# Input projection of a hybrid decoder layer: x stored by quarters, its loads and combinations in the order of the products, four sums on GpSimd

## The chip, the cores and the metric

One core of one Trainium2 chip runs the whole kernel as one program. The metric is device time in microseconds of that core. Its engines are called as the profile calls them: PE is TensorE (PEld its weight loads), DVE is VectorE, ACT is ScalarE, POOL is GpSimd, SP is SyncE, which here issues every DMA.

## The reference

The reference is one decoder layer for 1024 prompt tokens and 8 sample tokens that share the weights. All of it is float32. The change touches the first product, the projection of x into all branches, and two cache copies at the end of the decode branch:

```
z = x @ w_in                       # (1032 tokens, 1024) x (1024, 7680)
xr, yr, q, k, v, xq, g = split(z)  # conv + RG-LRU, window attention, memory attention, gates
...
s_win_k = concat(win_k, k)[:, -128:]   # 8 samples: the cached rows moved up by one, the new row last
s_win_v = concat(win_v, v)[:, -128:]
```

After z come the three branches, a gated merge, an output projection with LayerNorm, and a SwiGLU block with LayerNorm.

## The kernel before, in words

**Projection.** z is made transposed, 60 tiles of 128 columns, taken in 30 units of two tiles (the list UNITS, numbered from 0: unit 0 is "xq 0", unit 1 "lru 0", unit 2 "gate 0", unit 3 "xq 1"; the queue of side work runs beside them). A unit multiplies a weight matrix of 2 x 2 blocks (two tiles, each cut in two along the contraction) with x cut in 2 x 2 blocks (halves kh of the contraction, halves th of the tokens). It uses a seven-product scheme in place of eight products: seven sums of weight blocks (`fast_quarter`, lines 190 to 201; tiles us, u) times seven sums of x blocks (`combos`, lines 157 to 183; tiles t, th, tl). The tokens of a half are done in two parts p = 0 and 1 of 258, so a "quarter" of x is 4 x 258 numbers in each of 128 partitions, 516 KB. Each operand is held as two float32r numbers, high and low: ACT casts the high part (line 71), DVE subtracts for the low part (line 72). A product is then three matmuls for each of four contraction steps (lines 212 to 214), 12 matmuls of 128 x 258, and a unit has 7 x 2 x 12 = 168.

**Start of the projection.** `project` loads the four weight blocks of unit 0 (line 82, tiles ur), then calls `combos` for p = 0 and for p = 1. Each call loads its four quarters of x (line 153) from the tensor xT, whose rows are laid out by 128-row tiles, so a quarter comes in runs of 258 numbers (1032 bytes). It then makes t1 = b11 - b12, t2 = -t1 - b22, t3 = b22 - b12, t4 = -t2 - b21 on DVE (lines 170, 173, 177, 181), and splits b11, t1, t2, b21, t3, b22, t4 into high and low, the operands of products 0 to 6. The order of calls is the order in which a scheduler at build time weighs them; it decides each engine's fixed order of instructions by its own estimate of times and by the free buffers of the pools (9 buffers for tiles of the size of a quarter, 6 for raw weight blocks). On the chip each engine then runs its list strictly in that order and waits on semaphores. At most eight of SP's DMAs are under way: a ninth waits for the one eight places before it.

**Side work.** When a unit is finished, its results go on: an xq unit is split and stored (lines 298 to 306) and starts a generator for the sample tokens' memory attention (`dec_mem`, lines 709 to 748: products of cached keys on DVE, line 724); an lru unit starts the conv and recurrence (`lru`, lines 633 to 697: convolution on DVE, lines 646 and 647; casts and gate matmuls by thirds of the tokens, tiles xch, xcl, g; activations, line 662). `pump` lets one step of each run beside each product of the later units.

**Cache copies.** `dec_win_scores` (line 768), traced long after the projection, issues two copies within DRAM of 1016 KB each (line 777: o_swk from cwk, o_swv from cwv). They depend on nothing, so the scheduler puts them early in SP's list. `tc.issue_after(i)` is a block that queues what is traced in it on the engine of instruction i behind i; `self.last_mm` is the last matmul traced.

Of the kernel before, what the change touches and what calls it, by code (L numbers as in the profile page):

```python
# [11 lines left out]
F32R = mybir.dt.float32r  # L12
AF = mybir.ActivationFunctionType
ALU = mybir.AluOpType
# [4 lines left out]
P = 128  # L19
D = 1024  # L20
KT = D // P
TP = 1024
NB = 8
T = TP + NB
CH = ((0, 384), (384, 384), (768, 264))
NM = 256
# [7 lines left out]
HT = T // 2  # L34
QN = T // 4
QS = 272
# [17 lines left out]
class Builder:  # L54
# [94 lines left out]
    def x_quarter(self, kh, th, p):  # L149

        t = self.zt(f"x{kh}{th}{p}")
        t0 = HT * th + QN * p
        self.x_loaded = self.nc.sync.dma_start(t.rearrange("p (k n) -> p k n", k=4),
                                               self.io["xT"][:, 4 * kh:4 * kh + 4, t0:t0 + QN]).ins
        return t

    def combos(self, p, quarter):

        nc = self.nc
        b11, b21, b12, b22 = quarter(0, 0, p), quarter(1, 0, p), quarter(0, 1, p), quarter(1, 1, p)  # L160
        out = []

        def keep(src, i):
            hi, lo = (self.tp.tile([P, 4, QS], F32R, tag="t", name=f"t{e}{i}_{p}", bufs=28) for e in "hl")
            self.split(hi[:, :, :QN], lo[:, :, :QN], src.rearrange("p (k n) -> p k n", k=4))
            out.append((hi, lo))

        keep(b11, 0)
        t1 = self.zt(f"t1_{p}")
        nc.vector.tensor_sub(t1, b11, b12)  # L170
        keep(t1, 1)
        t2 = self.zt(f"t2_{p}")
        nc.vector.scalar_tensor_tensor(t2, t1, -1.0, b22, op0=ALU.mult, op1=ALU.subtract)
        keep(t2, 2)
        keep(b21, 3)
        t3 = self.zt(f"t3_{p}")
        nc.vector.tensor_sub(t3, b22, b12)
        keep(t3, 4)
        keep(b22, 5)
        t4 = self.zt(f"t4_{p}")  # L180
        nc.vector.scalar_tensor_tensor(t4, t2, -1.0, b21, op0=ALU.mult, op1=ALU.subtract)
        keep(t4, 6)
        return out

    def fast_load(self, u, src0, src1):
        h = D // 2
        return {"raw": [[self.half_raw(src[:, e * h:(e + 1) * h], h, f"ur{u}_{j}{e}") for e in range(2)]
                        for j, src in enumerate((src0, src1))], "u": u}

    def fast_quarter(self, st, i):  # L190

# [64 lines left out]
    def project(self):  # L256

        nc, io, tc = self.nc, self.io, self.tc
        self.qdc = self.cst.tile([P, KT * NB], F32, name="qdc")
        self.qds = self.cst.tile([P, KT * NB], F32, name="qds")  # L260
        self.kd = self.cst.tile([P, 2 * NB], F32, name="kd")
        self.vd = self.cst.tile([NB, 256], F32, name="vd")
        self.lru_setup()
        self.side, self.pumped = (deque(), deque()), 0
        n = len(UNITS)
        finish = [Finish(self, kind, j) for kind, j in UNITS]
        st = {}

        def load(u):
            a, b = finish[u].rows  # L270
            st[u] = self.fast_load(u, io["win"][a], io["win"][b])

        load(0)
        ts = [self.combos(p, self.x_quarter) for p in range(2)]
        with tc.issue_after(self.x_loaded):
            self.load_consts()
            self.load_lru()
        self.lru_consts()
        todo = [(u, i) for u in range(n) for i in range(7)]
        ahead = 3  # L280
        for u, i in todo[:ahead]:
            self.fast_quarter(st[u], i)
        for k, (u, i) in enumerate(todo):
            if i == 1 and u + 1 < n:
                load(u + 1)
            if k + ahead < len(todo):
                v, j = todo[k + ahead]
                self.fast_quarter(st[v], j)
            self.fast_step(st[u], i, ts, finish[u])
            self.pump()  # L290
            if i == 6:
                del st[u]
        while any(self.side):
            self.pump()
        nc.sync.dma_start(self.scr["c"][:, :, TP:T], self.cdec)
        self.store_lru()
# [471 lines left out]
    def dec_win_scores(self):  # L768

        nc, io, dp = self.nc, self.io, self.dp  # L770
        krow = dp.tile([NB, 256], F32, tag="krow", name="krow", bufs=1)
        ps = self.bank("mm", "dkt")
        for m in range(2):
            nc.tensor.transpose(ps[:NB, m * P:(m + 1) * P], self.kd[:, m * NB:(m + 1) * NB], self.ident)
        nc.scalar.copy(krow, ps[:NB, :256])
        for name, cache, row in (("o_swk", "cwk", krow), ("o_swv", "cwv", self.vd)):
            nc.sync.dma_start(io[name][:, 0:P - 1, :], io[cache][:, 1:P, :])
            nc.sync.dma_start(io[name][:, P - 1, :], row)
        qb = dp.tile([P, P], F32, tag="dqb", name="dqb", bufs=1)
        nc.gpsimd.memset(qb, 0.0)  # L780
        q5 = qb.rearrange("p (b j e g) -> p b j e g", b=NB, j=2, e=2)
        self.dec_heads(q5, self.qds.rearrange("p (m b) -> p m b", b=NB), True)
        sc = self.bank("mm", "dss")[:, :P]
        for b in range(NB):
            kk = dp.tile([P, 2, P], F32, tag="dk", name=f"dsk{b}", bufs=2)
            nc.sync.dma_start(kk, io["cwkT"][b])
            nc.gpsimd.tensor_copy(kk[:, :, 0], self.kd.rearrange("p (m b) -> p m b", b=NB)[:, :, b])
            for j in range(2):
                o = slice(b * 16 + 8 * j, b * 16 + 8 * j + 8)
                nc.tensor.matmul(sc[:, o], kk[:, j, :], qb[:, o], start=True, stop=True)  # L790
        self.dec_sc = dp.tile([P, P], F32, tag="dss", name="dss", bufs=1)
        nc.scalar.copy(self.dec_sc, sc)
# [307 lines left out]
class Finish:  # L1100
# [40 lines left out]


_INS = {
    "xT": (P, KT, T), "memT": (P, KT * NM), "wmk": (KT, P, D), "wmv": (8, P, D), "win": (60, P, D),
    "wbr": (24, P, D), "wout": (KT, P, D), "wgu": (2 * NF, P, D), "wdn": (KT, P, NF * P), "wlru": (KT, P, 256),
    "vec": (P, V_N), "cst": (P, P + 256), "scv": (P, KT, 3, NB), "sh": (P, KT, NB), "cwk": (NB, P, 256),
    "cwv": (NB, P, 256), "cwkT": (NB, P, 2, P), "cmk": (NB, NM, D), "cmvT": (NB, D, NM),
# [8 lines left out]
def _pack(i):  # L1156
    import numpy as np

    f = {k: np.asarray(v) for k, v in i.items()}
# [11 lines left out]
    o = {}  # L1171
    x = np.concatenate([f["x_prompt"].reshape(TP, D), f["x_sample"].reshape(NB, D)], axis=0)
    o["xT"] = x.T.reshape(KT, P, T).transpose(1, 0, 2)
    o["memT"] = f["mem_prompt"].reshape(NM, D).T.reshape(KT, P, NM).transpose(1, 0, 2).reshape(P, KT * NM)
    wkv = f["w_mem_kv"][0]
    o["wmk"] = mtiles(wkv[:, :D])
    o["wmv"] = np.concatenate([halves(wkv[:, D + 256 * n:D + 256 * (n + 1)]) for n in range(4)], axis=0)
    win = f["w_in"][0]
# [64 lines left out]
```

## Time and profile before

| | |
|---|---|
| median of 3 runs | 2022.97 us (2019.1 to 2027.29) |
| the profiled execution's own time | 2021.07 us |
| its span in the trace | 2018.5 us |
| unit 0's first matmul starts at | 10.00 us |
| unit 2's first matmul starts at | 68.79 us |
| granted TensorE clock, mean over the span | 0.993 |

A row of a timeline gives start, duration, engine, line, operation, output and inputs, shape, count, and in brackets how long the engine was idle before it and what ended that idle time. A row of the groups gives busy time and mean duration of one. A row of the windows gives, for a stretch of time, the busy time and number of operations of each engine, then the granted clock of TensorE, the share of time in which the DMA engines moved data, and GB/s. Matmul durations in the rows overlap; start to start is what counts.

### The profile page before, as it was taken

What the parts mean: (1) busy time and instruction counts of PE and PEld (TensorE: products, weight loads), DVE (VectorE), ACT (ScalarE), POOL (GpSimd) and SP (SyncE); (2) the same over time, 40 slices, a digit from 0 to 9 for tenths busy, and PEclk for the clock granted to TensorE, in tenths of its full rate; (3) what the DMA queues carried; (4) which work ended last, traced back from release to release, by engine and by line L of the source; (5) the groups of instructions that cost most, each with busy time, mean ns of one, the idle gap of its engine ahead of it and who ended that gap; (6) DMA issues with size and microseconds to landing.
All of it is one profiled execution on the core that took longest, in us unless ns stands there. A gap on an engine that the chain in (4) does not pass through costs nothing.

```text
span 2018.5 us, 35388 instructions
## 1 busy us (share of the span) xinstructions
PE 1960.8 (97%) x13732; PEld 1928.1 (96%) x13732; DVE 1198.8 (59%) x2569; ACT 878.8 (44%) x1922; POOL 112.7 (6%) x160
## 2 busy tenths in 40 slices
PE   6999999999999899999999999999999999999997
PEld 5999999999999898988999999999999999999996
DVE  8797789777766555399776559523222332233457
ACT  5456555646655455298673344322111221122324
POOL 1000010100000000022110003100000000000001
PEclk9999999999999999999999999999999999999998
DMA  5555544462233777567425241111211111111102
GB/s 196 186 170 176 184 155 163 150 225 103 95 132 122 248 226 225 158 168 208 136 85 171 88 136 29 42 42 49 57 42 43 48 54 45 55 42 43 57 29 84
DMA packets 143513, 235.42 MB, mean 117 GB/s; under 512 B 17281, under 2 KB 73681, under 8 KB 143313
## 3 DMA queue, kind: packets, MB, share of 16 engines
q1 hardware_dynamic: 143344, 233.17, 36.5%
q8 instruction: 107, 1.75, 0.4%
q14 instruction: 62, 0.50, 0.1%
HBM read 179.95 MB, written 55.23 MB: 117 GB/s over the span
## 4 chain that ended last, share of the span: by engine, by line
PE 85%; DVE 5%; DMA 5%; ACT 3%; issue 1%; SPq 0%; ACTq 0%; DVEq 0%; POOL 0%; POOLq 0%
PE ub L213 5%; PE ub L214 5%; PE ub L212 5%; PE fg L105 4%; PE fg L106 4%; PE fg L107 4%; PE fu L107 4%; PE fu L105 4%; PE fu L106 4%; PE d L105 3%; PE d L107 3%; PE d L106 3%; PE ud L214 2%; PE ud L213 2%; PE ud L212 2%; PE brs L105 2%
## 5 line engine op out<-in xcount | busy, mean ns | idle before, releaser
L105 PE MATMUL fg<-hH,wfg_h 128*128 128x384 f32 (+1 forms) x528 | 168.3, 319 | 2.9 <-DVE acc L978 1.7
L106 PE MATMUL fg<-hL,wfg_h 128*128 128x384 f32 (+1 forms) x528 | 167.7, 318 | 0.4 <-DVE hL L989 0.4
L107 PE MATMUL fu<-hH,wfu_l 128*128 128x384 f32 (+1 forms) x528 | 167.7, 318 | 0.0
L106 PE MATMUL fu<-hL,wfu_h 128*128 128x384 f32 (+1 forms) x528 | 167.6, 317 | 0.0
L105 PE MATMUL fu<-hH,wfu_h 128*128 128x384 f32 (+1 forms) x528 | 167.5, 318 | 0.0
L107 PE MATMUL fg<-hH,wfg_l 128*128 128x384 f32 (+1 forms) x528 | 167.5, 317 | 0.0
L1007 DVE TENSOR_TENSOR ft<-ft,fu 128x384 f32<-128x384 f32 (+1 forms) x66 | 33.8, 513 | 139.2 <-PE fu L107 139.1
L105 PE MATMUL d<-gH,wd_h 128*128 128x384 f32 (+1 forms) x360 | 114.4, 318 | 0.0
L1005 DVE SCALAR_TENSOR_TENSOR ft<-ft,fg 128x384 f32<-128x384 f32 (+1 forms) x66 | 33.8, 512 | 135.4 <-ACT ft L1004 133.3
L106 PE MATMUL d<-gL,wd_h 128*128 128x384 f32 (+1 forms) x360 | 114.2, 317 | 0.0
L107 PE MATMUL d<-gH,wd_l 128*128 128x384 f32 (+1 forms) x360 | 114.2, 317 | 0.0
L71 ACT CAST gH<-ft 128x384 fp32r<-128x384 f32 (+1 forms) x66 | 31.7, 480 | 174.8 <-DVE ft L1007 174.7
L105 PEld LDWEIGHTS fg<-hH,wfg_h 128*128 128x128 f32 x528 | 99.1, 188 | 3.9 <-DVE acc L978 2.0
L106 PEld LDWEIGHTS fg<-hL,wfg_h 128*128 128x128 f32 x528 | 99.2, 188 | 1.0 <-DVE hL L989 0.9
L107 PEld LDWEIGHTS fg<-hH,wfg_l 128*128 128x128 f32 x528 | 99.3, 188 | 0.0
L107 PEld LDWEIGHTS fu<-hH,wfu_l 128*128 128x128 f32 x528 | 99.2, 188 | 0.0
L105 PEld LDWEIGHTS fu<-hH,wfu_h 128*128 128x128 f32 x528 | 99.2, 188 | 0.0
L106 PEld LDWEIGHTS fu<-hL,wfu_h 128*128 128x128 f32 x528 | 99.2, 188 | 0.0
L1027 DVE SCALAR_TENSOR_TENSOR acc<-d,acc 128x384 f32<-128x384 f32 (+1 forms) x48 | 24.8, 516 | 108.4 <-PE d L107 108.4
L1004 ACT ACTIVATE ft<-fg 128x384 f32<-128x384 f32 (+1 forms) x66 | 30.1, 456 | 135.2 <-PE fg L107 135.2
L212 PE MATMUL ub<-th,u_0h 128*128 128x258 f32 x240 | 69.4, 289 | 15.5 <-ACT th L71 13.5
L212 PE MATMUL ud<-th,u_1h 128*128 128x258 f32 x240 | 69.4, 289 | 2.1 <-ACT th L71 1.4
(953 smaller groups left out, 6854.4 us busy)
## 6 DMA issues: line engine op xcount, KB each, us to landing
ur<-win SPq DMA_DIRECT2D x120, 256.0 KB, 2.7
dck<-cmk SPq DMA_DIRECT2D x32, 256.0 KB, 3.8
dcv<-cmvT SPq DMA_DIRECT2D x32, 256.0 KB, 3.9
st<-scr_q SPq DMA_DIRECT2D x32, 256.0 KB, 5.3
scr_g<-za SPq DMA_DIRECT2D x12, 516.0 KB, 4.1
scr_g<-zb SPq DMA_DIRECT2D x12, 516.0 KB, 5.1
x<-xT SPq DMA_DIRECT2D x8, 516.0 KB, 7.3
scr_a<-ge SPq DMA_DIRECT2D x8, 516.0 KB, 3.2
```

Of the source, the lines that this page charges most:

```text
L71: ins = self.nc.scalar.copy(hi, src).ins
L105: nc.tensor.matmul(ps, sh, mh, start=i == 0, stop=False)
L106: nc.tensor.matmul(ps, sh, ml, start=False, stop=False)
L107: self.last_mm = nc.tensor.matmul(ps, sl, mh, start=False, stop=closes and i == last).ins
L212: mm(sh[:, w], xh, start=opens and k == 0, stop=False)
L213: mm(sh[:, w], xl, start=False, stop=False)
L214: self.last_mm = mm(sl[:, w], xh, start=False, stop=k == 3).ins
L1004: nc.scalar.activation(t, pg, AF.Tanh, scale=0.5)
L1005: nc.vector.scalar_tensor_tensor(t, t, 1.0, pg, op0=ALU.add, op1=ALU.mult)
L1007: nc.vector.tensor_mul(t, t, pu)
L1027: nc.vector.scalar_tensor_tensor(a, ps, 0.5, a, op0=ALU.mult, op1=ALU.add)
```

## The change

x is stored a second time in DRAM, as xQ, where each quarter is contiguous: each partition's 1032 numbers are one run of 4128 bytes. One call of `combos` now serves both parts p. It asks for the loads and the sums in the order in which the products need them: the block of weights of product 0 and both quarters b11, then the blocks of the second row and b12, and so on, with the first three weight sums traced between. t3 is made before t2, t2 is made with its sign turned as t2n = t3 + b11, and the sign is put back when it is split (`split_scaled`, ACT multiply and DVE scalar_tensor_tensor). The four sums of part p = 1 are issued on GpSimd. The two cache copies stand in an `issue_after` block. The number of matmuls and splits is the same.

```
 def x_quarter(self, kh, th, p):
-    t0 = HT * th + QN * p
-    self.x_loaded = self.nc.sync.dma_start(t.rearrange("p (k n) -> p k n", k=4),
-                                           self.io["xT"][:, 4 * kh:4 * kh + 4, t0:t0 + QN]).ins
+    self.x_loaded = self.nc.sync.dma_start(t, self.io["xQ"][kh, 2 * th + p]).ins
...
+def combos(self, load, quarter):
...
+    def keep(i, p, src, sign=1.0):
+        hi, lo = (a[:, :, :QN] for a in ts[p][i])
+        src = src.rearrange("p (k n) -> p k n", k=4)
+        if sign < 0:
+            self.split_scaled(hi, lo, src, sign)
+        else:
+            self.split(hi, lo, src)
...
+    def both(op, name, p, a, b):
+        t[p][name] = self.zt(f"{name}_{p}")
+        (nc.gpsimd if p else nc.vector).tensor_tensor(t[p][name], a, b, op)
+    load(0)
+    quarter(0)
+    fetch((0, 0))
+    for p in range(2):
+        keep(0, p, raw[p][0, 0])
+    load(1)
+    quarter(1)
+    fetch((0, 1))
+    for p in range(2):
+        both(ALU.subtract, "t1", p, raw[p][0, 0], raw[p][0, 1])
+        keep(1, p, t[p]["t1"])
+    fetch((1, 1))
+    quarter(2)
+    for p in range(2):
+        both(ALU.subtract, "t3", p, raw[p][1, 1], raw[p][0, 1])
+        both(ALU.add, "t2n", p, t[p]["t3"], raw[p][0, 0])
+        keep(2, p, t[p]["t2n"], -1.0)
+    load(3)
+    fetch((1, 0))
+    for p in range(2):
+        keep(3, p, raw[p][1, 0])
+    for p in range(2):
+        keep(4, p, t[p]["t3"])
+        keep(5, p, raw[p][1, 1])
+        both(ALU.subtract, "t4", p, t[p]["t2n"], raw[p][1, 0])
+        keep(6, p, t[p]["t4"])
...
 # project
-    ts = [self.combos(p, self.x_quarter) for p in range(2)]
+    parts = {0: ((0, 0),), 1: ((1, 0), (1, 1)), 3: ((0, 1),)}
+    ts = self.combos(lambda i: st[0]["load"](*parts[i]), lambda i: self.fast_quarter(st[0], i))
...
-    for u, i in todo[:ahead]:
-        self.fast_quarter(st[u], i)
...
 # dec_win_scores
-    nc.sync.dma_start(io[name][:, 0:P - 1, :], io[cache][:, 1:P, :])
+    with self.tc.issue_after(self.last_mm):
+        nc.sync.dma_start(io[name][:, 0:P - 1, :], io[cache][:, 1:P, :])
```

More of the change, by code (lines that the diff above doesn't have):

```diff
@@ L151, in x_quarter @@
         t = self.zt(f"x{kh}{th}{p}")
-        t0 = HT * th + QN * p
-        self.x_loaded = self.nc.sync.dma_start(t.rearrange("p (k n) -> p k n", k=4),
-                                               self.io["xT"][:, 4 * kh:4 * kh + 4, t0:t0 + QN]).ins
+        self.x_loaded = self.nc.sync.dma_start(t, self.io["xQ"][kh, 2 * th + p]).ins
         return t
-    def combos(self, p, quarter):
+    def combos(self, load, quarter):
         nc = self.nc
[L160 to L183, printed above, removed]
@@ new lines, in combos @@
+        ts = [[None] * 7, [None] * 7]
+        for i in reversed(range(7)):
+            for p in range(2):
+                ts[p][i] = tuple(self.tp.tile([P, 4, QS], F32R, tag="t", name=f"t{e}{i}_{p}", bufs=28) for e in "hl")
+        raw, t = [{}, {}], [{}, {}]
+        def keep(i, p, src, sign=1.0):
[5 more added lines that the diff above has]
+                self.split(hi, lo, src)
@@ new lines, in fetch @@
+        def fetch(*where):
+            for p in range(2):
+                for kh, th in where:
+                    raw[p][kh, th] = self.x_quarter(kh, th, p)
+        def both(op, name, p, a, b):
[9 more added lines that the diff above has]
+        fetch((0, 1))
@@ new lines, in combos @@
+        for p in range(2):
[9 more added lines that the diff above has]
+        fetch((1, 0))
+        for p in range(2):
+            keep(3, p, raw[p][1, 0])
+        for p in range(2):
+            keep(4, p, t[p]["t3"])
+            keep(5, p, raw[p][1, 1])
+            both(ALU.subtract, "t4", p, t[p]["t2n"], raw[p][1, 0])
+            keep(6, p, t[p]["t4"])
@@ L185, in fast_load, with load @@
+        return ts
     def fast_load(self, u, src0, src1):
         h = D // 2
-        return {"raw": [[self.half_raw(src[:, e * h:(e + 1) * h], h, f"ur{u}_{j}{e}") for e in range(2)]
-                        for j, src in enumerate((src0, src1))], "u": u}
+        st = {"raw": [[None, None], [None, None]], "u": u}
+        def load(*halves):
+            for j, e in halves:
+                src = (src0, src1)[j]
+                st["raw"][j][e] = self.half_raw(src[:, e * h:(e + 1) * h], h, f"ur{u}_{j}{e}")
@@ L190, in fast_quarter @@
+        st["load"] = load
+        return st
     def fast_quarter(self, st, i):
@@ L271, in load @@
             st[u] = self.fast_load(u, io["win"][a], io["win"][b])
+            if u:
+                st[u]["load"]((0, 0), (0, 1), (1, 0), (1, 1))
         load(0)
-        ts = [self.combos(p, self.x_quarter) for p in range(2)]
+        parts = {0: ((0, 0),), 1: ((1, 0), (1, 1)), 3: ((0, 1),)}
+        ts = self.combos(lambda i: st[0]["load"](*parts[i]), lambda i: self.fast_quarter(st[0], i))
         with tc.issue_after(self.x_loaded):
@@ L1143 @@
 _INS = {
-    "xT": (P, KT, T), "memT": (P, KT * NM), "wmk": (KT, P, D), "wmv": (8, P, D), "win": (60, P, D),
+    "xT": (P, KT, T), "xQ": (2, 4, P, 4 * QN), "memT": (P, KT * NM), "wmk": (KT, P, D), "wmv": (8, P, D), "win": (60, P, D),
     "wbr": (24, P, D), "wout": (KT, P, D), "wgu": (2 * NF, P, D), "wdn": (KT, P, NF * P), "wlru": (KT, P, 256),
@@ L1173, in _pack @@
     o["xT"] = x.T.reshape(KT, P, T).transpose(1, 0, 2)
+    o["xQ"] = x.T.reshape(2, 4, P, 4, QN).transpose(0, 3, 2, 1, 4).reshape(2, 4, P, 4 * QN)
     o["memT"] = f["mem_prompt"].reshape(NM, D).T.reshape(KT, P, NM).transpose(1, 0, 2).reshape(P, KT * NM)
```

## The prediction

> **What bounds the kernel now.** I read the page first (engine shares and the chain), then the windows, the waits of PE over the first 70 us, the groups of DVE by form from 8 to 44 us, and timelines.
>
> ```profile
> span 2018.5 us, 35388 instructions
> ...
> PE 1960.8 (97%) x13732; PEld 1928.1 (96%) x13732; DVE 1198.8 (59%) x2569; ACT 878.8 (44%) x1922; POOL 112.7 (6%) x160
> ...
> PE 85%; DVE 5%; DMA 5%; ACT 3%; issue 1%; SPq 0%; ACTq 0%; DVEq 0%; POOL 0%; POOLq 0%
> ```
>
> PE is busy for 1960.8 of 2018.5 us and carries 85% of the chain. The change alters no matmul. It can only move the 58 us in which PE stands still, and matmuls at a low clock. The windows show where these are; I cut them at the first matmul of unit 0 (10.0), at the end of the x work (44), at the first matmul of unit 2 (68.8) and around a stall behind it.
>
> ```profile
> 0.00:10.00 10.00, 0.00 (x0) 0.00 (x0) 3.43 (x8) 3.62 (x5) 0.19 (x4) 1.00 0.81 253
> 10.00:44.00 34.00, 23.99 (x131) 21.95 (x132) 31.11 (x41) 18.96 (x28) 6.65 (x8) 0.90 0.62 212
> 44.00:68.80 24.80, 24.80 (x210) 24.75 (x209) 16.63 (x48) 9.79 (x21) 0.31 (x2) 1.00 0.47 161
> 71.60:75.40 3.80, 2.04 (x10) 1.11 (x9) 3.30 (x9) 2.41 (x5) 0.00 (x0) 1.00 0.00 0
> 75.40:79.00 3.60, 3.60 (x18) 3.60 (x19) 3.60 (x13) 1.32 (x4) 0.00 (x0) 0.53 0.31 94
> ```
>
> From 10 to 44 us PE gets 131 matmuls done in 34 us, and DVE is busy for 31.1 of them: **DVE sets the pace of the start**. From 44 on, PE runs 210 in 24.8 us, 0.118 us each, with nothing to gain. From 71.6 to 79 there is a small second stall (10 matmuls in 3.8 us, then 18 in 3.6 us at a granted clock of 0.53, 0.20 us each). So the change is worth what it does to the first 44 us, plus what it does to a stall like that one in a later unit.
>
> ```profile
> PE ub L212 <- ACT th L71: 14.0, 3, 10.0
> ```
>
> 10.0 us are lost until the first operand th exists, and 4.0 in two further places.
>
> **The start, part by part.** How soon can PE begin?
>
> ```profile
> 3.38 0.62 ACT L71 CAST u_0h<-ur 128x512 fp32r<-128x512 f32 x1 [1.39 <-DMA ur<-win]
> 8.89 1.05 ACT L71 CAST th<-x 128x1032 fp32r<-128x1032 f32 x1
> ```
>
> The first weight block is there at 3.38; three more blocks (768 KB) come ahead of the first x, which is there at 8.89. After the change only one block is ahead of b11. At the window's 253 GB/s its 516 KB take 2.0 us, so x is there at about 5.4, its cast ends at 6.5: the first matmul comes 3.5 us earlier. The longer runs of xQ are credited with nothing of their own: b11 (p = 0) is the only transfer with no other work in front, and the rate taken is the one that the old layout shared. Below, 0 and 0.6 us are the ends for it (0.6: a rate a third higher).
>
> But DVE sets the pace. What it has to do in the start:
>
> ```profile
> L72 DVE TENSOR_TENSOR tl<-t,th 128x1032 fp32r<-128x1032 f32 x8 | 9.8, 1227 | 0.1
> L72 DVE TENSOR_TENSOR tl<-x,th 128x1032 fp32r<-128x1032 f32 x6 | 7.4, 1231 | 1.2 <-ACT th L71 1.2
> L170 DVE TENSOR_TENSOR t<-x,x 128x1032 f32<-128x1032 f32 x2 | 2.5, 1230 | 0.6 <-DMA x<-xT 0.6
> L173 DVE SCALAR_TENSOR_TENSOR t<-t,x 128x1032 f32<-128x1032 f32 x2 | 2.4, 1224 | 0.0
> L177 DVE TENSOR_TENSOR t<-x,x 128x1032 f32<-128x1032 f32 x2 | 2.4, 1224 | 0.0
> L181 DVE SCALAR_TENSOR_TENSOR t<-t,x 128x1032 f32<-128x1032 f32 x2 | 2.4, 1224 | 0.0
> ```
>
> 22 operations of 128x1032, 14 splits and 8 sums. Two back to back start 1.15 us apart, and the last split of the start begins at 41.28 and ends at 42.5:
>
> ```profile
> 18.93 1.23 DVE L72 TENSOR_TENSOR tl<-x,th 128x1032 fp32r<-128x1032 f32 x1
> 20.08 1.23 DVE L181 SCALAR_TENSOR_TENSOR t<-t,x 128x1032 f32<-128x1032 f32 x1
> 41.28 1.23 DVE L72 TENSOR_TENSOR tl<-t,th 128x1032 fp32r<-128x1032 f32 x1
> ```
>
> The four sums that leave DVE save 4 x 1.15 = 4.6 us there. t2n with its sign turned costs the same instruction form as before (L173 and L72 have one duration), so it is costed at nothing.
>
> **What four sums on GpSimd do to DVE.** This trace has two places where both engines read SBUF at once:
>
> ```profile
> 2005.79 2.77 DVE L952 TENSOR_TENSOR acc<-acc,lmu 128x264 f32<-128x264 f32 x3
> 2005.74 4.12 POOL L952 TENSOR_TENSOR acc<-acc,lmu 128x264 f32<-128x264 f32 x5 [3.09 <-ACT lmu L948]
> L952 POOL TENSOR_TENSOR acc<-acc,lmu x5: 737/927/933, 2005.7 to 2009.1; 128x264 f32<-128x264 f32 x5
> 613.72 1.23 DVE L679 SCALAR_TENSOR_TENSOR ti<-ti,sq 128x1032 f32<-128x1032 f32 x1
> 613.93 1.94 POOL L677 TENSOR_SCALAR tr<-th 128x1032 f32<-128x1032 f32 x1 [59.53 <-DVE sq L676]
> 614.87 1.53 DVE L72 TENSOR_TENSOR u_4l<-us,u_4h 128x512 fp32r<-128x512 f32 x1
> 616.33 0.68 DVE L72 TENSOR_TENSOR u_5l<-us,u_5h 128x512 fp32r<-128x512 f32 x1
> ```
>
> At 614.87 a weight split takes 1.53 us where the next one, u_5l, takes 0.68. It ends at 616.40, 0.53 after the end of POOL's operation at 615.87: it waited for that end. POOL's took 1.94, and counted from the end of the DVE operation before it (614.95) 0.92. The two took turns. At 2005.8 the same: three DVE operations beside POOL take 0.92 each (2.77 / 3), as long as POOL's 0.93. So I read: **a DVE operation with two SBUF inputs is held until POOL's running one ends**, and back.
>
> How long is a POOL sum of 128x1032? No row shows it.
>
> ```profile
> L787 POOL COPY dsk<-kd 128x2 f32<-128x2 f32 x8 | 1.6, 196 | 86.6 <-DMA dsk<-cwkT 84.3 <-PE dss L790 2.3
> L677 POOL TENSOR_SCALAR tr<-th x8: 1062/1491/2036, 124.5 to 613.9; 128x1032 f32<-128x1032 f32 x8
> ```
>
> Below: 1.06 us, the shortest operation with one input of that size. Above: 0.737 x 1032 / 264 = 2.88. With a fixed part of 0.2 (a POOL copy of two columns) the 0.737 leaves 0.54 for 264 columns, so 0.2 + 0.54 x 1032 / 264 = 2.3. I take 2.3, worked out from the only two-input row. The Trainium skill, page "GPSIMD Engine Reference", section 3.1, gives 4497 ns for an add of 2048 float32 columns; halved by size that is an estimate of 2.27 us, and the sum would be the same. Its section 1 says that GPSIMD shares its SBUF interfaces with VectorE and contends with DVE instructions that have two SBUF inputs, a rule that speaks against this edit; the rows at 614.87 and 2005.79 agree.
>
> In the built order of the changed kernel DVE's next operation behind each such sum has two SBUF inputs: u_1l behind t1 of p = 1, t3 of p = 0, t2n of p = 0, and a low split behind t4. All four wait in full: 4 x 2.3 = 9.2 us.
>
> Two more terms. In the built order six operations of 512 columns (0.69 each; sums and splits of weights, three of them for unit 1) stand inside the stretch that were behind or in idle time before: +3.6 net of 0.6 that fell in idle time. And 2.1 us of waits inside the stretch vanish, as x and weights now come in the order of use (0.6 and 1.2 in the group rows, the rest in front of weight sums). Sum for the last x split: -3.5 - 4.6 - 2.1 + 3.6 + 9.2 = **+2.6 us**, at 45.1.
>
> PE: before, unit 2 starts 26.3 us behind that split's end (68.8 - 42.5). In the order of the products p = 0 and p = 1 alternate, so what is left of unit 0 behind the last split is its last product, some two dozen matmuls fewer: 23 x 0.118 = 2.7 us. Start: 2.6 - 2.7 = **-0.1, taken as 0**.
>
> **The cache copies and unit 3.** In the built order the copy of o_swk goes from place 17 to 25 of SP's list, o_swv from 27 to 39, behind more loads. They are 1016 KB each and free DMA time early (shares 0.62 and 0.47 from 10 to 68.8 us, and the PE waits there are on ACT and DVE): nothing gained. But the scheduler also lays out other work anew. In unit 3 ("xq 1") its first weight sum us stood ahead of unit 1's conv work on DVE. In the changed order it stands behind the low split xcl of the last third of that lru tile and behind four products of cached keys. Prices from the like place in unit 2:
>
> ```profile
> L662 ACT ACTIVATE ti<-g,lruc 128x344 f32<-128x344 f32 x3 | 1.6, 548 | 0.0
> 71.30 0.28 PE L212 MATMUL ub<-th,u_0h 128*128 128x258 f32 x1
> 71.42 0.28 PE L213 MATMUL ub<-tl,u_0h 128*128 128x258 f32 x1
> 71.97 0.48 ACT L71 CAST xch<-xc 128x344 fp32r<-128x344 f32 x1 [1.10 <-DVE xc L646]
> 72.48 0.52 DVE L72 TENSOR_TENSOR xcl<-xc,xch 128x344 fp32r<-128x344 f32 x1 [0.46 <-ACT xch L71]
> 72.91 0.69 DVE L196 TENSOR_TENSOR us<-ur,ur 128x512 f32<-128x512 f32 x1
> 73.64 0.62 ACT L71 CAST u_1h<-us 128x512 fp32r<-128x512 f32 x1 [0.91 <-DVE us L196]
> 74.25 0.42 DVE L724 SCALAR_TENSOR_TENSOR dcj<-dck,dcq 128x256 f32<-128x256 f32 x1
> ```
>
> xch waits on ACT behind the activation ti (0.55, of which 0.45 counts), which waits for g's matmuls, queued on PE behind product 0 of unit 3. So PE has finished product 0 and waits for product 1's weights: 0.45 + 0.48 (xch) + 0.52 (xcl) + 4 x 0.43 (cached keys) + 0.69 (us) + 0.62 (u_1h) = 4.5 us, then about 1.0 for u_1l behind the next sum: 5.5 idle. After an idle stretch of 3.8 us in unit 2 came 18 matmuls at 0.20 instead of 0.118 (window 75.4 to 79): 18 x 0.08 = 1.5 more. Unit 3: **+7.0 us**. Its ends: 0 (the wait ends early because the casts run sooner, or the key products' operands come with them) to 9 (two such slow stretches). Behind it PE has no slack to catch up: a gap in front of 97% busy PE stays to the end.
>
> **Sum.** 0 + 7.0 on the profiled execution's 2021.07 (span 2018.5 and 2.6 around it) gives 2028; that execution is 1.9 below the median of 2022.97, so the forecast for the median is **2030 us**.
>
> **Rivals.** (a) No hold: DVE and POOL run beside one another. The 9.2 us go, against it stand the two timelines. PE is then limited by ACT and the loads, about 8 us gained in all, and unit 3 still stalls: 2030 - 8 = 2022. (b) No stall in unit 3, the order not biting because the activations come earlier than PE's queue makes me think: 2023. (c) Both: 2015. A sum on POOL of 1.06 us lies between (a) and the forecast (2030 - 5 = 2025), one of 2.88 gives 2032. (d) Slower: POOL's first sum starts late, because POOL has to fetch the program for it.
>
> ```profile
> L677 POOLq MODIFY_POOL_CONFIG  x2: 11/11/11, 66.9 to 67.0; - x2
> ...
> x<-xT SPq DMA_DIRECT2D x8, 516.0 KB, 7.3
> ```
>
> Before, that instruction stands at 66.9 and the first operation behind it starts at 124.5, so any load was hidden. In the built order it stands at POOL's start, some 10 us ahead of the first sum: the rival decides only if the fetch begins with the first call. A fetch among the x loads would take up to the 7.3 us that these take to land, and at least 0; at 5.5 every one of them delays t1 of p = 1, on which DVE's list waits: 2030 + 5.5 = 2035.5. The Trainium skill, same page, section 2.1, says that the first call to a freshly loaded kernel pays about 6 us without a visible instruction; by that figure it would be 2036, and no run so far shows it. (e) The block for the cache copies does nothing by itself: it queues only instructions of the named matmul's engine, and the copies are SP's. They move because the rest was laid out anew. Worth nothing either way, and no case of its own.
>
> **How the numbers follow.** Forecast (2025 to 2034 with the ends of the POOL sum and the slow clock) 0.50; (a) 0.12; (b) 0.12; (c) 0.12; (d) 0.08; anything else 0.06, half on each side. A measurement of this kernel tells 0.5% (10.1 us) from no change: faster means under 2012.9, slower over 2033.1. Faster: under half of (c) and half of the rest, 0.08. Slower: a fifth of the forecast, most of (d), half of the rest, 0.20. Same: 0.72. The range leaves out the lower half of (c), the upper half of (d) and the rest: 2014 to 2036.
>
> **What would show it.** Right: first matmul near 6.5; POOL sums of about 2.3 us with DVE operations of 2.4 us or more beside them; unit 2's first matmul near 69; a gap of PE of 4 to 5 us behind unit 3's product 0, ended by ACT's u_1h; unit 4's first matmul about 7 later than before. Wrong: DVE rows of 1.2 us beside POOL's (a); no such gap (b); a POOL sum that starts well behind its last input (d).

## The result, and the profile after

| | before | changed |
|---|---|---|
| median of 10 runs | 2020.74 us (2017.25 to 2027.29) | 2029.59 us (2027.84 to 2033.78) |
| ratio to before | | 1.0043, 95% interval 1.0031 to 1.0055 |
| span of the profiled execution | 2018.5 us | 2027.6 us |

The changed kernel is 0.43% slower, 8.7 us on the median of before. First matmuls of the units, read from PE's timelines (us from the start of the span):

| first matmul of unit | 0 | 2 | 3 | 4 | 5 | 7 |
|---|---|---|---|---|---|---|
| before | 10.00 | 68.79 | 94.67 | 116.49 | 136.60 | 180.04 |
| changed | 6.07 | 68.72 | 93.11 | 124.70 | 144.98 | 189.72 |

So the lead of 3.9 us at the first matmul is gone at unit 2, 1.5 us are won in unit 2, and 9.8 are lost in unit 3. Behind that the two run nearly alike (9.7 us apart at unit 7, 9.1 in the spans). The page of the changed kernel:

```profile
span 2027.6 us, 35380 instructions
...
PE 1963.3 (97%) x13732; PEld 1930.0 (95%) x13732; DVE 1204.2 (59%) x2565; ACT 879.1 (43%) x1922; POOL 125.3 (6%) x164
...
PE 86%; DVE 6%; DMA 3%; ACT 3%; issue 1%; SPq 0%; ACTq 0%; DVEq 0%; POOL 0%; POOLq 0%
```

The shares hardly differ: 9 us in 2028 are not to be seen there. The waits of PE in the first 70 us show that one wait was traded for others:

```profile
PE ub L244 <- ACT th L71: 6.1, 1, 6.1
PE ub L244 <- ACT th L77: 5.4, 1, 5.4
PE ud L245 <- DVE tl L72: 3.1, 1, 3.1
```

The wait for the first x block is down from 10.0 to 6.1 us, but PE now waits 5.4 us for t2n's high part and 3.1 us for t1's low part. What these waited for stands in DVE's and POOL's timelines of the changed kernel:

```profile
10.92 1.23 DVE L180 TENSOR_TENSOR t<-x,x 128x1032 f32<-128x1032 f32 x1
12.06 2.87 DVE L72 TENSOR_TENSOR u_1l<-us,u_1h 128x512 fp32r<-128x512 f32 x1
14.85 0.68 DVE L72 TENSOR_TENSOR u_2l<-us,u_2h 128x512 fp32r<-128x512 f32 x1
...
18.94 3.43 DVE L180 TENSOR_TENSOR t<-x,x 128x1032 f32<-128x1032 f32 x1
...
22.89 3.38 DVE L180 TENSOR_TENSOR t2n<-t,x 128x1032 f32<-128x1032 f32 x1
...
32.83 3.25 DVE L72 TENSOR_TENSOR tl<-x,th 128x1032 fp32r<-128x1032 f32 x1 [0.15 <-ACT th L71]
```

```profile
11.71 2.66 POOL L180 TENSOR_TENSOR t<-x,x 128x1032 f32<-128x1032 f32 x1 [11.29 <-DMA x<-xQ]
18.50 2.78 POOL L180 TENSOR_TENSOR t<-x,x 128x1032 f32<-128x1032 f32 x1 [4.12 <-DVE tl L72]
22.50 2.68 POOL L180 TENSOR_TENSOR t2n<-t,x 128x1032 f32<-128x1032 f32 x1 [1.22 <-issue]
31.76 3.23 POOL L180 TENSOR_TENSOR t<-t2n,x 128x1032 f32<-128x1032 f32 x1 [6.57 <-DVE t L180]
```

Each long DVE row has a POOL row beside it. u_1l needs nothing from POOL, yet takes 2.87 us where u_2l behind it takes 0.68, and ends 0.56 us after POOL's sum.

Windows of the changed kernel around the gap in unit 3 (columns as before: PE, PEld, DVE, ACT, POOL, then clock, DMA share, GB/s):

```profile
93.11:96.60 3.49, 3.49 (x29) 3.23 (x27) 0.00 (x0) 1.50 (x4) 0.00 (x0) 1.00 0.00 0
96.60:101.20 4.60, 0.05 (x2) 0.02 (x1) 3.45 (x11) 1.53 (x3) 0.00 (x0) 0.90 0.19 57
101.20:104.90 3.70, 3.33 (x14) 3.03 (x15) 2.17 (x7) 1.14 (x2) 0.00 (x0) 0.50 0.91 305
104.90:108.30 3.40, 3.40 (x22) 3.40 (x22) 3.32 (x9) 1.94 (x5) 0.00 (x0) 0.67 0.88 297
108.30:113.00 4.70, 3.22 (x28) 2.98 (x27) 3.02 (x11) 1.88 (x5) 0.00 (x0) 1.00 0.81 273
```

While PE does product 0 of unit 3 (93.1 to 96.6), DVE does nothing at all. Then PE stands still and DVE works. The timelines of DVE, ACT and PE at that place say why:

```profile
97.61 0.52 DVE L72 TENSOR_TENSOR xcl<-xc,xch 128x344 fp32r<-128x344 f32 x1 [7.23 <-ACT xch L71]
98.04 0.42 DVE L757 SCALAR_TENSOR_TENSOR dcj<-dck,dcq 128x256 f32<-128x256 f32 x1
...
99.79 0.69 DVE L228 TENSOR_TENSOR us<-ur,ur 128x512 f32<-128x512 f32 x1
```

```profile
96.66 0.55 ACT L695 ACTIVATE ti<-g,lruc 128x344 f32<-128x344 f32 x1
97.11 0.47 ACT L71 CAST xch<-xc 128x344 fp32r<-128x344 f32 x1
100.51 0.62 ACT L71 CAST u_1h<-us 128x512 fp32r<-128x512 f32 x1 [2.93 <-DVE us L228]
```

```profile
96.31 0.32 PE L107 MATMUL g<-xch,wgl 128*128 128x344 f32 x1
101.18 0.58 PE L244 MATMUL ud<-th,u_1h 128*128 128x258 f32 x1 [4.55 <-ACT u_1h L71]
```

DVE waited 7.23 us for xch at the head of its list, with four cached-key products and unit 3's weight sum ready behind. xch stood on ACT behind the activation ti, ti waited for PE (the gate matmuls g behind product 0, the last at 96.31), and PE then waited for that sum.

### The profile page after: what moved, and what is told of

The parts are those of the page before. It is cut to its first block, busy times and chain, and to the rows that moved or that the text cites. A ratio compares the mean times of both kernels' runs of the same rounds, so it can differ in the third digit from the quotient of the medians.

```text
span 2027.6 us, 35380 instructions
## 1 busy us (share of the span) xinstructions
PE 1963.3 (97%) x13732; PEld 1930.0 (95%) x13732; DVE 1204.2 (59%) x2565; ACT 879.1 (43%) x1922; POOL 125.3 (6%) x164
## 4 chain that ended last, share of the span: by engine, by line
PE 86%; DVE 6%; DMA 3%; ACT 3%; issue 1%; SPq 0%; ACTq 0%; DVEq 0%; POOL 0%; POOLq 0%
PE ub L245 5%; PE ub L244 5%; PE ub L246 5%; PE fg L105 4%; PE fg L106 4%; PE fg L107 4%; PE fu L107 4%; PE fu L105 4%; PE fu L106 4%; PE d L105 3%; PE d L107 3%; PE d L106 3%; PE ud L246 2%; PE ud L245 2%; PE ud L244 2%; PE brs L105 1%
```

## The experiments

The theory: (1) POOL's sums hold DVE, which takes away what four sums fewer and an earlier start give; (2) the order built for unit 3 costs the rest. The rivals: DVE waits for POOL's results and not for POOL; the loads or the copies make the gap. "n1" to "n12" are in the order in which they ran; the ratio is always to the kernel before on the same chip.

**n1: all eight sums on DVE.**

```
-        (nc.gpsimd if p else nc.vector).tensor_tensor(t[p][name], a, b, op)
+        nc.vector.tensor_tensor(t[p][name], a, b, op)
```

> The changed kernel with all eight sums of x blocks on DVE. My theory: the four DVE operations that stood beside POOL's sums took 2.87, 3.43, 3.38 and 3.25 us in place of 0.68, 1.23, 1.23 and 1.23, so 8.6 us of holds go and 4 x 1.15 = 4.6 us of sums come back to DVE: unit 2's first matmul about 4 us earlier than the 68.7 of the changed kernel, near 64.7. In the built order the first weight sum of unit 3 stands ahead of the lru work again, so the 4.55 us gap of PE in unit 3 goes too, with the slow clock and the 1.5 us wait of the score transposes behind it (9.8 us from unit 3's to unit 4's first matmul more than before): 2029.6 - 4 - 9.8 = 2016 us (2012 to 2019). Rival, POOL's sums cost DVE nothing: the start gets 4.6 us longer, unit 2 near 73.3, and 2029.6 + 4.6 - 9.8 = 2024. Rival, the stall in unit 3 comes from late weight loads and not from DVE's order: it stays, 2025 to 2026.

Measured: 2014.74 us, ratio 0.9979 (0.9970 to 0.9988), faster than both kernels. Unit 2 starts at 66.19, unit 4 at 113.43. The start gained 2.5 us of the 4 expected, since DVE in n1's start stands idle for 2.3 us in all behind PE and ACT. Unit 3 takes 21.8 us, as before. The rival at 2024 is out. n1 undoes two things at once, for the scheduler built unit 3 anew; so n2 leaves the sums on POOL.

**n2: only unit 3's order.** In `lru`, for tile 0 and the second third of the tokens (us1 is the weight sum of product 1 traced last):

```
-            self.split(xch, xcl, xc[:, t0:t0 + n])
+            if (m, c) == (0, 1):
+                nc.scalar.copy(xch, xc[:, t0:t0 + n])
+                with self.tc.issue_after(self.us1):
+                    nc.vector.tensor_sub(xcl, xc[:, t0:t0 + n], xch.bitcast(F32))
+            else:
+                self.split(xch, xcl, xc[:, t0:t0 + n])
```

> The changed kernel, sums on POOL kept, with only the low split of the second third of unit 1's lru tile put on DVE behind unit 3's first weight sum; the cached-key products then do not wait for it either. My theory: the start is as in the changed kernel (unit 2's first matmul at 68.7), the gap of 4.55 us behind unit 3's product 0 goes, unit 4's first matmul comes near 115 in place of 124.7, and the time is 2029.6 - 9.8 = 2020 us (2017 to 2023), no different from the kernel before. Rival, loads: unit 3's blocks or the cached keys land late whatever DVE does, the gap stays at 2 us or more and the time is 2026 or more.

Measured: 2021.74 us, ratio 1.0014 (1.0005 to 1.0023). The start is unchanged (unit 2 at 69.26), the 4.55 us gap and the slow clock behind it are gone (granted clock 1.00 in all of unit 3), and unit 4 starts at 118.47, 6.2 earlier than in the changed kernel and 3.5 later than expected. Unit 3 still takes 25.1 us where it took 21.8 before; 2.05 of the 3.3 between them are three small waits of PE:

```profile
97.36 0.39 PE L246 MATMUL ud<-th,u_1h 128*128 128x258 f32 x1 [0.67 <-ACT u_1h L71]
98.08 0.39 PE L248 MATMUL ud<-th,u_1l 128*128 128x258 f32 x1 [0.22 <-DVE u_1l L72]
105.01 0.27 PE L770 MATMUL dct<-ident,dcs 128*8 128x128 f32 x1 [1.16 <-DVE dcj L764]
```

So the order, not the loads, made the gap.

**n3: x from xT.** The load reads `xT[:, 4 * kh:4 * kh + 4, t0:t0 + QN]` again; everything else is the changed kernel.

> The changed kernel with x loaded from xT in runs of 1032 bytes, as before; every engine's order is the same. My theory: the longer runs are worth at most 0.6 us at the first x block and nothing behind it, since DVE sets the pace: first matmul between 6.1 and 6.7, 2030 us (2028 to 2032). Rival, the layout carries the early first matmul: first matmul 1 us or more later, and the time 2032 or more.

Measured: 2028.96 us, ratio 1.0049 (1.0035 to 1.0063); first matmul at 6.20, 0.13 later than in the changed kernel. The layout by quarters is worth nothing that can be measured here.

**n4: the kernel before, two sums on POOL.**

```
-        nc.vector.tensor_sub(t1, b11, b12)
+        (nc.gpsimd if p else nc.vector).tensor_sub(t1, b11, b12)
```

and the same for t3.

> The kernel before with t1 and t3 of p = 1 on POOL and nothing else; unit 3's order stays as before. My theory: each sum holds DVE's next two-input operation about 2.2 us and saves DVE 1.15, so unit 2's first matmul comes 2 us later (70.8 for 68.8), and the time is 2020.7 + 2 = 2023 us (2020 to 2025). Rival, no hold: 2.3 us earlier, unit 2 at 66.5, 2018.5.

Measured: 2019.04 us, ratio 0.9999 (0.9990 to 1.0008): a miss. Unit 2 starts at 69.47, 0.7 later than before and not 2.0, and unit 4 at 116.49 as before: unit 2 won 1.5 us, at a granted clock of 1.00 where the kernel before has 18 matmuls at 0.53, and unit 3 lost 0.8. In its timeline of DVE:

```profile
29.99 0.82 DVE L72 TENSOR_TENSOR u_4l<-us,u_4h 128x512 fp32r<-128x512 f32 x1 [2.83 <-PE ub L214]
30.73 3.42 DVE L173 SCALAR_TENSOR_TENSOR t<-t,x 128x1032 f32<-128x1032 f32 x1
```

The second sum held DVE for 2.2 us (3.42 for 1.22). The first ran while DVE stood idle for 2.83 us waiting for PE to free a buffer, and cost nothing. A hold costs only where DVE has something to do.

**n5: POOL sums that nobody needs.** n1, and before t1, t3 and t2n of p = 1 a POOL sum of the same inputs into the buffer of the last low part, which is overwritten later. The result is not used:

```
+            if p and name != "t4":
...
+                nc.gpsimd.tensor_tensor(spare, k4(a), k4(b), op)
+            nc.vector.tensor_tensor(t[p][name], a, b, op)
```

> The kernel with all eight sums on DVE (n1), and besides three sums of 128x1032 on POOL, with the inputs of t1, t3 and t2n of p = 1, into a buffer that is overwritten before it is read: nothing waits for their results, and DVE's list is the same as in n1. My theory (a two-input DVE operation is held until POOL's running one ends): each holds DVE about 2.2 us, 6.6 in all, less what falls into DVE's idle time (2.3 us in n1's start): unit 2's first matmul between 70 and 73 in place of 66.2, time 2014.7 + 4 to 7 = 2019 to 2022. Rival (in the changed kernel DVE waited for POOL's results, not for POOL): unit 2 at 66.2, 2014.7.

Measured: 2023.15 us, ratio 1.0024 (1.0015 to 1.0033), against n1's 0.9979. Unit 2 starts at 72.43, 6.2 later than in n1. DVE's rows of n5:

```profile
11.79 2.88 DVE L72 TENSOR_TENSOR u_1l<-us,u_1h 128x512 fp32r<-128x512 f32 x1
...
16.88 2.88 DVE L72 TENSOR_TENSOR u_2l<-us,u_2h 128x512 fp32r<-128x512 f32 x1
...
25.46 3.40 DVE L78 SCALAR_TENSOR_TENSOR tl<-t2n,th 128x1032 fp32r<-128x1032 f32 x1
```

Three operations, each 2.2 us longer than its own 0.68 or 1.23, with no data from POOL to wait for. Apart from the three sums, the traces of n1 and n5 have the same operations in the same order on every engine, to the end of the program. This shows the hold as a cause by itself, and rules out the rival. The time rose by 0.45%, some 9 us. The two traces are 6.2 us apart from unit 2 to unit 7 and 7.6 at the end (spans 2013.6 and 2021.2); where the rest comes from was not traced.

**n6: POOL copies.** As n5 with `nc.gpsimd.tensor_copy(spare, k4(b))`.

> As n5, with POOL copies (one input of 128x1032) in place of the three sums. My theory: an operation with one input holds DVE too, for as long as it lasts, at least 1.06 us each: unit 2's first matmul 1 to 4 us behind n1's 66.2, 2016 to 2019. Rival (only two inputs on POOL contend): no DVE operation longer than its usual 1.23, 66.2, 2014.7.

Measured: 2017.62 us, ratio 0.9999 (0.9990 to 1.0008); unit 2 at 68.82, 2.6 us later than in n1. DVE's rows of n6:

```profile
12.23 1.53 DVE L72 TENSOR_TENSOR u_1l<-us,u_1h 128x512 fp32r<-128x512 f32 x1
13.68 2.07 DVE L184 TENSOR_TENSOR t<-x,x 128x1032 f32<-128x1032 f32 x1
15.67 2.07 DVE L72 TENSOR_TENSOR tl<-t,th 128x1032 fp32r<-128x1032 f32 x1
```

Each is 0.85 us longer, less than the 1.06 expected: an operation with one input on POOL holds DVE too, for less.

**n7 and n8: the copies really late.** In the changed kernel the `issue_after(self.last_mm)` block binds nothing: the trace has the copies issued at 29.1 and 60.3 us, while the row that is stored right behind the first of them in the program (o_swk from krow) goes at 741.3. The named instruction is one of PE, the copies are SP's. n7 is n1, n8 the changed kernel, with a load as the named instruction:

```
-            with self.tc.issue_after(self.last_mm):
+            with self.tc.issue_after(self.last_load):
```

> n1 with the two cache copies queued on SP's list behind the load that was traced last, so that they are issued some hundred microseconds later in the program. In the built order unit 2's first weight sum then stands on DVE ahead of the lru work that it waited behind. My theory: unit 2's stall (1.8 us of idle and 18 matmuls at a clock of 0.53, 1.4 us) goes: unit 3's first matmul near 88.5 in place of 91.6, 2014.7 - 3 = 2012 us (2010 to 2014). Rival: the stall is set by the conv itself or moves to a later unit: 2014.7.

> The changed kernel, sums on POOL kept, with the copies late as in n7. In the built order unit 3's first weight sum then stands ahead of the lru work. My theory: the start is the changed kernel's (unit 2 at 68.7), unit 3's 9.8 us and unit 2's stall (about 1.5 us) go: 2029.6 - 10 to 11.5 = 2018 to 2020. Rival: the order of the copies does not matter for unit 3, 2028 to 2030.

Measured: n7 2020.22 us, ratio 1.0014 (1.0005 to 1.0022); n8 2024.23 us, ratio 1.0030 (1.0018 to 1.0043). Both a miss as times. The stages did what was expected: n7 reaches unit 4 at 108.22, 5.2 ahead of n1, and n8 at 112.24, 12.5 ahead of the changed kernel. n7 gave it all back in the memory attention, where its copies are now issued, at 701.8 and 725.0. The rows of the attention's first and last products, of n1 and then of n7:

```profile
L105 PE MATMUL co<-cph,mvh x32: 389/397/504, 730.7 to 830.6; 128*128 128x512 f32 x32
```

```profile
L105 PE MATMUL co<-cph,mvh x32: 387/398/797, 719.5 to 833.7; 128*128 128x512 f32 x32
```

11.2 us ahead at the first, 3.1 behind at the last. n8 lost as much there: it is 16.5 us ahead of the changed kernel at the first of these products (725.0 and 741.5) and 1.4 at the last (841.7 and 843.1). So I asked whether the transfers did that or the order built there.

**n9, n10, n11: the copies in the feed-forward block.** The copies are taken out of `dec_win_scores` and stand behind the weight loads of feed-forward tiles 4 and 6, in n1, in the kernel before, and in the changed kernel:

```
                 wu = self.weights(io["wgu"][NF + f], D, f"wfu{f}")
+                if f in (4, 6):
+                    name, cache = {4: ("o_swk", "cwk"), 6: ("o_swv", "cwv")}[f]
+                    with self.tc.issue_after(self.last_load):
+                        nc.sync.dma_start(io[name][:, 0:P - 1, :], io[cache][:, 1:P, :])
```

> n1 (all sums on DVE) with the two cache copies queued behind weight loads of the feed-forward block, where the DMA engines are busy for about 15% of the time. n7 was 5 to 6.5 us ahead of n1 from unit 4 to unit 9 and gave it all back between 672 and 1063 us, where its copies ran beside the loads of the memory attention. Theory A (the copies' transfers did that): here the lead stays, 2014.7 - 5 to 6.5 = 2008 to 2010. Theory B (the other order that the scheduler built in that part did it, or the lead meets a later wait): 2012 to 2018.

> The kernel before with nothing changed but the copies queued in the feed-forward block. The built order of unit 2 is then that of n7, its stall (3.2 us) goes, and SP's early loads come sooner. Theory A as for n9: 4 to 6 us faster than the kernel before. Theory B: within 2 us of it, or slower.

> The changed kernel, sums on POOL kept, with the copies queued in the feed-forward block. n8 had no stall in unit 3 and was 11.8 us ahead of the changed kernel in unit 9, then lost 8. Theory A: 2029.6 - 11 = 2018 to 2020. Theory B: 2022 to 2026. In both, the start is the changed kernel's (unit 2 near 68.8), since POOL's holds are still there.

Measured: n9 2015.27 us, ratio 0.9989 (0.9980 to 0.9997); n10 2017.09, ratio 0.9995 (0.9986 to 1.0004); n11 2020.56, ratio 1.0012 (1.0003 to 1.0021). By the times theory B for n9 and n10, and n11 between the two. The stages say otherwise: the lead now survives the memory attention, and goes in the feed-forward block, in front of whose weights the copies stand. (The order of PE's products in the memory attention is another one in n7 than in n9, so whether the transfers or the order cost n7 its lead stays open.) The rows of its first and last products, of n1 and then of n9:

```profile
L105 PE MATMUL fg<-hH,wfg_h x528: 280/334/441, 1249.6 to 1911.4; 128*128 128x384 f32 x132, 128*128 128x264 f32 x44
```

```profile
L105 PE MATMUL fg<-hH,wfg_h x528: 280/334/444, 1245.2 to 1911.3; 128*128 128x384 f32 x132, 128*128 128x264 f32 x44
```

n1 takes 661.8 us from one to the other, n9 666.1. Of these 4.3 us, 3.0 are a wait that n1 does not have:

```profile
PE fg L105 <- ACT wfg_h L71: 3.0, 2, 1.5
```

Two waits, one behind each copy. n10 and n11 lose the same 4 us there. But the loads behind the copy were not late. The first of them in n9, with the cast that PE waited for and the operation ahead of it on ACT:

```profile
1313.86 0.34 SPq L82 DMA_DIRECT2D wfg5r__17191<-wgu  x1
1359.99 0.41 ACT L71 CAST gH<-ft 128x264 fp32r<-128x264 f32 x1 [2.93 <-DVE ft L1039]
1360.31 0.61 ACT L71 CAST wfg_h<-wfg5r__17191 128x512 fp32r<-128x512 f32 x1
```

The load is issued at 1313.86, just behind the copy. From 1322 to 1333 the DMA engines stand still (share of 0.00), so it had landed more than 30 us before its cast began. The cast came late because it stands on ACT's list behind gH, which waited for PE. The second wait, at the next pair of loads, is alike (load at 1363.50, cast at 1407.40 behind gH at 1407.09).

**n12: the copies behind the last weight load.** n1 with the copies queued behind the last load of the down projection, where nothing is loaded after them.

> n1 (all sums on DVE) with the two cache copies queued behind the last weight load of the kernel, where nothing loads behind them any more. In n9 the lead of the start and the middle (4.4 us at the first feed-forward product) was given back in the feed-forward block, where PE waited 3.0 us for weight casts of the blocks queued behind the copies. Theory A (a copy costs where loads with a due time are queued behind it): the feed-forward block is back to n1's 662.1 us from its first to its last product, the lead stays, 2015.3 - 4.2 = 2011 us, 6 to 8 us faster than the kernel before. Theory B (the loss in the feed-forward block was an effect of the order built there): 2014 to 2016.

Measured: 2011.90 us, ratio 0.9959 (0.9945 to 0.9972). The feed-forward row of n12:

```profile
L105 PE MATMUL fg<-hH,wfg_h x528: 280/334/441, 1244.9 to 1906.8; 128*128 128x384 f32 x132, 128*128 128x264 f32 x44
```

661.9 us again, and the lead stays to the end. The same cast has moved with the copies, to 1336.69 and in front of gH:

```profile
1336.69 0.62 ACT L71 CAST wfg_h<-wfg5r__17190 128x512 fp32r<-128x512 f32 x1 [0.84 <-PE fu L106]
1337.28 0.41 ACT L71 CAST gH<-ft 128x264 fp32r<-128x264 f32 x1
```

So the time is that of theory A, and the reason for the waits is that of theory B: the order of ACT's casts, which the scheduler built otherwise around the copies. Why it did is not shown. This is the best version: 8 us faster than the kernel before and about 17 faster than the changed one.

## Why the prediction was right

It forecast 2030 us; 2029.59 were measured. The median of before, taken again, was 2020.74 and not 2022.97, so the change was worth +8.7 us where the sum had +7: the kernel before was taken some 2 us too slow and the change nearly 2 us too small. That 2030 was met within half a microsecond is luck; the direction and the two mechanisms are not. Step by step:

- **First matmul** at 6.5: it came at 6.07. That earlier loads gain nothing by themselves held; n3 adds that the layout is worth nothing.
- **POOL's sum** of 2.3 us: the four rows read 2.66 to 3.23, but counted from the end of the DVE operation already under way, as the prediction counted the row at 613.93, they are 2.2 to 2.3. In n4, where DVE stood idle, one took 2.38. The size was right. **The holds**, 9.2 us for four: (2.87 - 0.68) + (3.43 - 1.23) + (3.38 - 1.23) + (3.25 - 1.23) = 8.6. Right, and shown as a cause by n5.
- **End of the last x split** at 45.1: 44.1. The 1.0 is the first matmul (0.4) and the holds (0.6). **Unit 2's first matmul** at the same time as before: 68.72 for 68.79. Here two errors cancel: from the last split to unit 2 PE took 24.6 us, 1.7 less than before and not 2.7.
- **Unit 3**, +7.0: the mechanism was right in each link (xch, xcl, four key products, us, u_1h, and 4.5 us of gap, 4.55 measured), the size was not: +9.8. Two things were missing. The clock stayed low twice as long as counted: 14 and 22 matmuls in the windows at 0.50 and 0.67, where 18 were counted. Cut by single microseconds, the low stretch is 6.8 us at 0.50 (100.3 to 107.1), against 3.4 us (75.5 to 78.9) in unit 2 of the kernel before. (The prediction put unit 2's slow clock behind "an idle stretch of 3.8 us". That is the length of the window; PE was busy for 2.04 of it.) And the key products, held up by DVE's wait, freed their buffers late, so that the next cached keys were loaded late and PE waited 1.5 us for their scores (the score transposes, dct, in the waits from 70 to 140 us):

```profile
PE ud L244 <- ACT u_1h L71: 5.2, 2, 4.5
PE dct L763 <- DVE dcj L757: 1.5, 1, 1.5
```

  The 1.0 us for u_1l, on the other hand, were 0.4. Gap, u_1l, slow clock (2.5, worked out at the end) and scores make 8.9 of the 9.8; the rest is not traced.

- **Unit 2**, not in the sum: -1.5. Its stall is still there (PE busy for 22.63 of 24.39 us), but at a granted clock of 1.00, where before 18 matmuls ran at 0.53. The window of unit 2 in the changed kernel:

```profile
68.72:93.11 24.39, 22.63 (x179) 21.70 (x178) 15.07 (x33) 10.63 (x22) 0.00 (x0) 1.00 0.17 55
```

  The gaps of PE in it are the same in both traces, 0.68, 0.67 and 0.28 us. Why they bring the clock down in one run and not in the other was not tried.
- **The cache copies** at nothing: right for the change as written, since its block binds nothing. What I left out is that with the place of the copies the scheduler builds another order elsewhere: n7 to n12 moved 4 to 12 us from stage to stage with it.
- **The rivals.** No hold (a): ruled out by n5. No gap (b) and both (c): the gap came. A late first sum on POOL (d): POOL's first sum starts at 11.71, released by the landing of x. The instruction that changes POOL's program stands at 0.7 us, so this trace cannot show a load that takes less than 11 us:

```profile
L180 POOLq MODIFY_POOL_CONFIG  x2: 11/11/11, 0.7 to 0.8; - x2
```

  The figure of about 6 us in the Trainium skill, page "GPSIMD Engine Reference", section 2.1, is neither confirmed nor contradicted. That the copies' block does nothing (e) held.

The Trainium skill, page "GPSIMD Engine Reference", section 1, speaks of contention for DVE instructions with two SBUF inputs. The measured form of it here is a wait in turn: 2.2 us per two-input sum of 128x1032, 0.85 per copy of that size (n5, n6).

## What to carry to other kernels

Work moved to POOL is not off DVE's path when the DVE operations beside it have two inputs in SBUF: count a hold for each POOL operation that meets such a DVE operation, and compare it with what the same operation takes on DVE (here 2.2 against 1.15 us), but nothing where DVE waits anyway (n4). Where a scheduler decides the order, a small edit changes the lists far behind it; read the built order for the first operation that a busy engine needs next and look at what stands ahead of it. And the place of a transfer without a due time is such an edit: in n9 the casts of the loads queued behind it moved on ACT's list and PE waited 3.0 us for them, though the loads had landed long before. Behind the last load (n12) it cost nothing.

## What was not expected of the hardware

A one-input POOL operation holds a two-input DVE operation as well, 0.85 us for 128x1032 (n6). The row at 614.87 of the kernel before had shown it already (1.53 for 0.68, beside a POOL operation with one input). A gap of PE of 4.55 us was followed by 7.1 us with a granted clock of 0.50 for most of the time, which cost about 2.5 us (36 matmuls in 7.1 us less the 0.4 of a wait, against 36 x 0.118); the gap's own length was not the whole price.
